# Transfers of the first input pair on two queues, squares of the stream after the last weight cast, and a split power of scales in a one-core decoder trunk

## The chip, the core and the metric

The kernel runs on one core of a Trainium2 chip. The metric is the device time in microseconds (us) of one execution, lower is better; it is given as the median of three runs. The engines are named as in the profile: PE is the matrix engine (TensorE), PEld its weight loads, DVE the VectorE, ACT the ScalarE, POOL the GpSimd engine, and SP the engine that only issues transfers here. Each engine executes its instructions in the order in which they stand in its queue. SP and ACT both issue DMA transfers, each on a queue of its own.

## What is computed

A two-layer decoder trunk on a sequence of 256 positions, width 1024. The first layer (DSA) projects the normalized stream with `w_in`, cuts the result into latents, and lets an indexer pick for each query the top 64 keys; everything that the change touches lies in these lines:

```python
h = rmsnorm(x, g_attn[0])
proj = h @ w_in                       # 1024 x 456
c_q, c_kv, k_idx, w_idx = split(proj, [256, 384, 448])
c_q, c_kv, k_idx = rmsnorm of each
q_idx = einsum(c_q, w_q_idx)
rel = relu(einsum(q_idx, k_idx)); score = einsum(w_idx, rel)   # causal mask
sel = top_k(score, 64)                # then attention over the chosen latents
x = x + attention @ w_o; x = x + sq_relu_mlp(rmsnorm(x), w_up, w_down)
# second layer (NSA), its MLP, final rmsnorm
```

## The kernel before

All 256 positions are held in on-chip memory, transposed (`xT`: 8 row blocks of 128 by 256). The program is one straight line: input projection, indexer, top-k, attention, output projection, MLP, the second layer. The order of the instructions on each engine is set by a scheduler with a cost model of its own; only instructions wrapped in `pin` keep the order in which they are written, and `behind(a, b)` puts `a` after `b`. Tiles come from pools; transfers signal completion on eight counters that are used in turn, so that the ninth transfer waits until the first has landed, and so on.

The **input stage** (L206 to L283) runs over four pairs j of row blocks. For each, SP brings a pair of `xT` (256 KB, written x0 to x3 below) and a pair of weight blocks `win{j}_raw` (456 KB, w0 to w3). SP's queue holds: `vec` (26 KB of gains, L207), then x0, w0, x1, w1, x2, w2, x3, w3 (L252, L254), `cst`, the next weights, `biasT`, and then the output weights `wo_raw`.

- Pair 0 is used in plain fp32: ACT scales x0 by the gain (`xg0`, L258, two instructions), and PE makes four matmuls of 456 columns (two rows each in the trace), called the first projection below.
- Pairs 1 to 3 are split into a high and a low part. ACT makes the high part of the stream pair (`xgh`, L260) and of the two weight blocks (`win`, L266, two instructions); DVE makes the low parts (`xgl` L261, `win` L267). PE makes 12 matmuls of 456 columns for each pair (`mm3`), 36 in all, called the split projection.
- ACT then squares the four stream pairs (`sqs`, L278), two of them ahead of the casts of w3. DVE adds the squares (L280) behind its last low part, POOL makes `Sx`.

At the start PE runs ten matmuls of `ones` by `ones` (`warm_ps`, 20 rows) and one small matmul `ups` for a bias table, which goes by DVE (`usb`), an ACT transfer (`udr`, L231) and an SP transfer (`biasT`, L301) to the attention.

After the projection DVE copies its query part (`zc`, L314), PE transposes it, DVE and ACT form the sums of squares `ss`, and POOL raises six of them per position to the power -0.5 in one instruction (`scs`, L355): columns 0 and 1 for the query and key/value latents, column 2 for the indexer keys. Another power follows (L356). With column 2 DVE scales the keys (`kd`, L362), PE transposes them (`tk`), DVE writes `kiT`, PE makes the indexer products `ix`, and DVE the scores and the top-k.

Of the kernel before, what the change touches and what calls it, by code (L numbers as in the profile page):

```python
# [22 lines left out]
F32 = mybir.dt.float32  # L23
F32R = mybir.dt.float32r
AF = mybir.ActivationFunctionType
OP = mybir.AluOpType
# [4 lines left out]
P, T, D, KT = 128, 256, 1024, 8  # L31
# [19 lines left out]
def trunk(ctx: ExitStack, tc: tile.TileContext, I, out):  # L51
    nc = tc.nc
    const = ctx.enter_context(tc.tile_pool(name="const", bufs=1))
    big = ctx.enter_context(tc.tile_pool(name="big", bufs=10))
    rawp = ctx.enter_context(tc.tile_pool(name="raw", bufs=5))
# [5 lines left out]
    def new_phase(name):  # L61
        nonlocal work
        phase.close()
        work = phase.enter_context(tc.tile_pool(name=name, bufs=2, reuse_waits="tile"))
# [5 lines left out]
    def bank(name, acc=False):  # L70
        if acc:
            return psA.tile([P, 512], F32, tag="acc", name=name)
        return psB.tile([P, 512], F32, tag="ps", name=name)

    def bigt(shape, dt, name):
        return big.tile(shape, dt, tag="big", name=name)

    def wk(tag, bufs, shape, name, dt=F32):
        return work.tile(shape, dt, tag=tag, name=name, bufs=bufs)
# [4 lines left out]
    def k4(shape, name, dt=F32):  # L84
        return rawp.tile(shape, dt, tag="raw", name=name)
# [4 lines left out]
    def f(ap):  # L90
        return ap.bitcast(F32)

    def mm(ps, a, b, start, stop):
        return nc.tensor.matmul(ps, a, b, start=start, stop=stop, skip_group_check=True)  # L94

    def mm3(ps, ah, al, bh, bl, start, stop):
        mm(ps, ah, bh, start, False)
        mm(ps, ah, bl, False, False)
        mm(ps, al, bh, False, stop)

    def behind(ins, prev):

        tc.add_manual_dep(ins.ins, prev.ins.name,
                          mybir.DependencyInfo(mybir.DependencyClass.NoSync, mybir.DependencyReason.DATA),
                          reason="order")
# [46 lines left out]
    def pin(ins):  # L152

        return tc.keep_in_program_order(ins)
# [48 lines left out]


    new_phase("workA")
    vec = const.tile([P, NV], F32, name="vec")  # L206
    nc.sync.dma_start(vec, I["vecs"])  # L207
    mhalf = const.tile([P, 4], F32, name="mhalf")
    nc.gpsimd.memset(mhalf, -0.5)
    ones = const.tile([P, P], F32, name="ones")  # L210
# [3 lines left out]
    wps = bank("warm_ps")  # L214
# [7 lines left out]

    ups = bank("ups")
    mm(ups[:H, :256], relb, oneh, True, True)
    for n in range(2):
        mm(wps[:, :P], ones, ones, True, True)
    usb = wk("pe", 4, [H, 384], "usb")
    nc.gpsimd.memset(usb[:, :P], NEG)
    nc.vector.tensor_copy(usb[:, P - 1:P + 255], ups[:H, :256])
# [9 lines left out]

    xT = bigt([P, KT, T], F32, "xT")
    xgh = bigt([P, KT, T], F32R, "xgh")
    xgl = bigt([P, KT, T], F32R, "xgl")
    proj = [bank(f"proj{i}", acc=True) for i in range(2)]
# [1 line left out]
    sqs = bigt([P, 4, 2, T], F32, "sqs")  # L247
    cst = const.tile([P, NC_], F32, name="cst")
    lo_last = None
    for j in range(4):  # L250
        pair = slice(2 * j, 2 * j + 2)
        nc.sync.dma_start(xT[:, pair], I["xT"][:, pair])  # L252
        raw = rawp.tile([P, 2, 456], F32, tag="raw", name=f"win{j}_raw")
        nc.sync.dma_start(raw.rearrange("p a m -> p (a m)"), I["a_w_in"][j])  # L254
        if j == 0:
            xg0 = k4([P, 2, T], "xg0")
            for k in range(2):
                nc.scalar.activation(xg0[:, k], xT[:, k], AF.Copy, scale=vec[:, V_GA + k:V_GA + k + 1])  # L258
        else:
            xh = nc.scalar.copy(xgh[:, pair], xT[:, pair])  # L260
            nc.vector.tensor_sub(xgl[:, pair], xT[:, pair], f(xgh[:, pair]))  # L261
            w = wp.tile([P, 2, 1024], F32R, tag="w", name=f"win{j}")
            wh, wl = (w[:, s, :912].rearrange("p (a m) -> p a m", a=2) for s in range(2))
            for a in range(2):
                g = vec[:, V_GA + 2 * j + a:V_GA + 2 * j + a + 1]
                hi_last = nc.scalar.activation(wh[:, a], raw[:, a], AF.Copy, scale=g)  # L266
                lo_last = nc.vector.scalar_tensor_tensor(wl[:, a], raw[:, a], g, f(wh[:, a]),  # L267
                                                         op0=OP.mult, op1=OP.subtract)
        for i in range(2):
            for a in range(2):  # L270
                k = 2 * j + a
                if j == 0:
                    mm(proj[i][:, :456], xg0[:, k, i * P:(i + 1) * P], raw[:, a], k == 0, False)
                    continue
                mm3(proj[i][:, :456], xgh[:, k, i * P:(i + 1) * P], xgl[:, k, i * P:(i + 1) * P],
                    wh[:, a], wl[:, a], False, k == KT - 1)
    for j in range(4):
        behind(nc.scalar.activation(sqs[:, j], xT[:, 2 * j:2 * j + 2], AF.Square), hi_last if j > 1 else xh)  # L278
    for j in range(1, 4):
        sq_last = nc.vector.tensor_tensor(sqs[:, 0], sqs[:, 0], sqs[:, j], op=OP.add)  # L280
        behind(sq_last, lo_last)
# [60 lines left out]
    ss = const.tile([P, 2, 4], F32, name="ss")  # L342
# [9 lines left out]
                                               accum_out=ss[:, i, j:j + 1])  # L352
        nc.vector.tensor_scalar(ss[:, i, :3], ss[:, i, :3], epv[:, i:i + 1], None, op0=OP.add)
    scs = const.tile([P, 2, 4], F32, name="scs")
    nc.gpsimd.tensor_tensor(scs[:, :, :3], ss[:, :, :3], mhalf[:, None, :3].to_broadcast([P, 2, 3]), op=OP.pow)  # L355
    pin(nc.gpsimd.tensor_tensor(scs[:, :, 3], msx, mhalf[:, :2], op=OP.pow))  # L356
    sc = [scs[:, i] for i in range(2)]
    indexer_queries(0)
# [513 lines left out]
    for kv in range(2):  # L872
        ps = bank(f"kc{kv}")
        for g in range(G):
# [7 lines left out]
                                      op=OP.mult)  # L882
# [84 lines left out]
    raw = rawp.tile([P, 1024], F32, tag="raw", name="wg_raw")  # L967
# [419 lines left out]
```

## Time and profile before

| | |
|---|---|
| median of three runs | 593.86 us (593.1 to 595.12) |
| profiled execution, device time | 593.29 us |
| its span, first to last instruction | 591.5 us |
| PE busy in the span | 577.2 us (98%) |
| DVE, ACT, POOL busy | 364.2, 320.4, 159.1 us |
| transfers | 103.97 MB, 176 GB/s over the span |

The profile has a page with busy times, 40 slices and the chain of work that ended last; the trace behind it gives every instruction with its start, its duration and what it waited for. Times in it are us from the start of the span. A row of the timeline reads: start, duration, engine, line, operation, out<-in, shape, count, and in brackets how long the engine was idle before and what ended that.

### The profile page before, as it was taken

To read this page: it belongs to the slowest core of one execution; us is meant where nothing else is said; L and a number is where in the kernel's file an instruction comes from. 1 tells how busy PE (TensorE), PEld (TensorE's weight loads), DVE (VectorE), ACT (ScalarE), POOL (GpSimd) and SP (SyncE) were. 2 spreads that over 40 slices of the span, in tenths; PEclk is the share of its full clock that TensorE was granted. 3 is DMA by queue.
4 is the path that set the end of the run, shared out by engine and by line. 5 is a ranking of instruction groups with operands and counts; after the bars stand their busy time and mean duration, and the time that the engine had idled before them with its cause. 6 is when DMAs were issued, how large, how long until landed. Compare 5 with 4: busy or idle time off the path is not lost.

```text
span 591.5 us, 10852 instructions
## 1 busy us (share of the span) xinstructions
PE 577.2 (98%) x4170; PEld 542.9 (92%) x4170; DVE 364.2 (62%) x612; ACT 320.4 (54%) x580; POOL 159.1 (27%) x225
## 2 busy tenths in 40 slices
PE   8899999999999999999999999999999999999995
PEld 6787899999999999999968999999899999999994
DVE  3897399544474444547897877639845444454523
ACT  6656666444444454436866878637544545454423
POOL 0155457010101011015530076808310110011012
PEclk9999999999999999999999999999999999999998
DMA  8911447765546656543499943314866665656201
GB/s 300 345 47 61 149 176 235 249 194 178 179 145 212 181 178 190 180 164 113 160 308 304 327 139 102 97 49 138 287 205 186 181 191 169 180 180 203 77 0 71
DMA packets 30475, 103.97 MB, mean 176 GB/s; under 512 B 3632, under 2 KB 5464, under 8 KB 30296
## 3 DMA queue, kind: packets, MB, share of 16 engines
q1 hardware_dynamic: 30024, 102.45, 53.7%
q10 hardware_dynamic: 400, 0.83, 0.5%
q8 instruction: 32, 0.52, 0.4%
q14 instruction: 19, 0.16, 0.1%
HBM read 102.21 MB, written 1.06 MB: 175 GB/s over the span
## 4 chain that ended last, share of the span: by engine, by line
PE 84%; DVE 9%; issue 2%; DMA 2%; ACT 1%; POOL 1%; SPq 1%; POOLq 0%; ACTq 0%; DVEq 0%
PE y L94 30%; PE u L94 28%; PE nq L94 4%; PE yb L94 3%; PE ya L94 3%; PE kk L94 2%; PE npo L94 2%; PE kc L94 1%; PE nl L94 1%; DVE c L903 1%; DMA win_raw<-in_a_w_in 1%; PE v L94 1%; PE co L94 1%; PE ix L94 1%; DMA wv_raw<-in_kvV 1%
## 5 line engine op out<-in xcount | busy, mean ns | idle before, releaser
L142 DVE TENSOR_TENSOR dn<-dn_raw,dn 128x1024 fp32r<-128x1024 f32 x64 | 80.6, 1260 | 99.2 <-ACT dn L141 99.2
L645 POOL TENSOR_TENSOR us<-ur 128x256 f32<-128x256 f32 x64 | 45.4, 711 | 282.0 <-ACT ur L642 282.0
L142 DVE TENSOR_TENSOR up<-up_raw,up 128x1024 fp32r<-128x1024 f32 x64 | 81.9, 1280 | 44.6 <-ACT up L141 44.6
L141 ACT CAST up<-up_raw 128x1024 fp32r<-128x1024 f32 x64 | 67.0, 1048 | 60.0 <-PE y L94 58.5
L94 PE MATMUL u<-h1h,up 128*128 128x256 f32 x512 | 97.0, 284 | 0.6 <-DVE up L142 0.6
L94 PE MATMUL y<-uu,dn 128*128 128x256 f32 x768 | 97.0, 283 | 0.3 <-DVE uu L647 0.3
L94 PE MATMUL u<-h0h,up 128*128 128x256 f32 x512 | 96.7, 283 | 0.0
L94 PEld LDWEIGHTS y<-uu,dn 128*128 128x128 f32 x768 | 94.2, 192 | 0.5 <-DVE uu L647 0.5
L94 PE MATMUL y<-dn,uu 128*128 128x512 f32 (+1 forms) x396 | 92.5, 384 | 0.0
L94 PEld LDWEIGHTS y<-dn,uu 128*128 128x128 f32 x396 | 71.1, 189 | 13.0
L94 PEld LDWEIGHTS u<-h1h,up 128*128 128x128 f32 x512 | 81.5, 191 | 1.6 <-DVE up L142 0.8
L642 ACT ACTIVATE ur<-u 128x256 f32<-128x256 f32 x64 | 24.6, 384 | 107.2 <-PE u L94 107.2
L94 PEld LDWEIGHTS u<-h0h,up 128*128 128x128 f32 x512 | 81.7, 192 | 0.0
L94 PE MATMUL u<-h1l,up 128*128 128x256 f32 x256 | 72.5, 283 | 0.0
L94 PE MATMUL u<-h0l,up 128*128 128x256 f32 x256 | 72.2, 283 | 0.0
L141 ACT CAST dn<-dn_raw 128x1024 fp32r<-128x1024 f32 x64 | 66.7, 1042 | 7.2 <-PE y L94 3.0
L94 PEld LDWEIGHTS u<-h1l,up 128*128 128x128 f32 x256 | 49.0, 191 | 0.9
L94 PEld LDWEIGHTS u<-h0l,up 128*128 128x128 f32 x256 | 49.1, 192 | 0.0
L647 DVE TENSOR_TENSOR uu<-us,uu 128x256 fp32r<-128x256 f32 x64 | 29.1, 455 | 8.1 <-POOL us L645 8.1
L646 ACT ACTIVATE uu<-ur 128x256 fp32r<-128x256 f32 x64 | 26.7, 417 | 0.1
L94 PE MATMUL ya<-oT,wo 128*128 128x256 f32 x192 | 25.2, 288 | 0.3 <-DVE oT L591 0.3
L94 PE MATMUL nq<-ah,wq 128*128 128x256 f32 x128 | 24.9, 286 | 0.0
(300 smaller groups left out, 966.8 us busy)
## 6 DMA issues: line engine op xcount, KB each, us to landing
up_raw<-in_w_up SPq DMA_DIRECT2D x64, 512.0 KB, 3.7
dn_raw<-in_w_down SPq DMA_DIRECT2D x64, 512.0 KB, 3.7
c1raw<-in_cmp_w SPq DMA_DIRECT2D x16, 512.0 KB, 4.9
wo_raw<-in_a_w_o SPq DMA_DIRECT2D x8, 512.0 KB, 4.1
wq_raw<-in_b_w_q SPq DMA_DIRECT2D x8, 512.0 KB, 5.9
wn_raw<-in_b_w_o SPq DMA_DIRECT2D x8, 512.0 KB, 4.9
wk_raw<-in_kvT SPq DMA_DIRECT2D x4, 512.0 KB, 3.6
wc_raw<-in_kvT SPq DMA_DIRECT2D x4, 512.0 KB, 3.6
```

The lines of the kernel that those rows point to most:

```text
L94: return nc.tensor.matmul(ps, a, b, start=start, stop=stop, skip_group_check=True)
L141: ins = [hi(w[:, 0, :C], raw[:, :C]) if hi else nc.scalar.copy(w[:, 0, :C], raw[:, :C]), (lo or nc.vector).tensor_sub(w[:, 1, :C], raw[:, ...
L142: (lo or nc.vector).tensor_sub(w[:, 1, :C], raw[:, :C], f(w[:, 0, :C]))]
L642: nc.scalar.activation(r, ps[:, :T], AF.Relu)
L645: nc.gpsimd.tensor_tensor(s, r, r, op=OP.mult)
L646: nc.scalar.activation(u[:, 0], r, AF.Square)
L647: nc.vector.tensor_sub(u[:, 1], s, f(u[:, 0]))
L903: lo = nc.vector.tensor_sub(w4[:, :, 1], r4, f(w4[:, :, 0]))
```

## The change

- x0 becomes the first transfer on SP. w0 becomes the first on ACT, and `vec` the second on ACT, behind it. In the order of the changed program SP then holds x1, x2, x3, and behind them w1, w2, w3.
- On PE three `ones` matmuls are pinned behind `ups` (two stood there before).
- All four squares stand behind the last high cast of w3 (`hi_last`).
- POOL's power is split: first the keys' column 2 for both halves (two values per partition), then columns 0 and 1 (four values), then the one of L356 as before.

```diff
+    xT = bigt([P, KT, T], F32, "xT")
+    pin(nc.sync.dma_start(xT[:, 0:2], I["xT"][:, 0:2]))
+    raw0 = rawp.tile([P, 2, 456], F32, tag="raw", name="win0_raw")
+    pin(nc.scalar.dma_start(raw0.rearrange("p a m -> p (a m)"), I["a_w_in"][0]))
     vec = const.tile([P, NV], F32, name="vec")
-    nc.sync.dma_start(vec, I["vecs"])
+    pin(nc.scalar.dma_start(vec, I["vecs"]))
...
-    for n in range(2):
-        mm(wps[:, :P], ones, ones, True, True)
+    for n in range(3):
+        pin(mm(wps[:, :P], ones, ones, True, True))
...
-        nc.sync.dma_start(xT[:, pair], I["xT"][:, pair])
-        raw = rawp.tile([P, 2, 456], F32, tag="raw", name=f"win{j}_raw")
-        nc.sync.dma_start(raw.rearrange("p a m -> p (a m)"), I["a_w_in"][j])
+        raw = rawp.tile([P, 2, 456], F32, tag="raw", name=f"win{j}_raw") if j else raw0
+        if j:
+            nc.sync.dma_start(xT[:, pair], I["xT"][:, pair])
+            nc.sync.dma_start(raw.rearrange("p a m -> p (a m)"), I["a_w_in"][j])
...
-        behind(nc.scalar.activation(sqs[:, j], xT[:, 2 * j:2 * j + 2], AF.Square), hi_last if j > 1 else xh)
+        behind(nc.scalar.activation(sqs[:, j], xT[:, 2 * j:2 * j + 2], AF.Square), hi_last)
...
-    nc.gpsimd.tensor_tensor(scs[:, :, :3], ss[:, :, :3], mhalf[:, None, :3].to_broadcast([P, 2, 3]), op=OP.pow)
+    pin(nc.gpsimd.tensor_tensor(scs[:, :, 2], ss[:, :, 2], mhalf[:, :2], op=OP.pow))
+    pin(nc.gpsimd.tensor_tensor(scs[:, :, :2], ss[:, :, :2], mhalf[:, None, :2].to_broadcast([P, 2, 2]), op=OP.pow))
```

The scheduler orders the changed program anew. The places where its order differs and that matter below are these.

On ACT, in the input stage, before (`xg` is the scaled x0, `xgh` the high part of x1, x2, x3 in turn; `win_134`, `win_156`, `win_178` are the high parts of w1, w2, w3):

```order
L218 DMA relb<-in_rel_bias 32x8
L213 ACTIVATE warm<-ones 128x1
L220 DMA oneh<-in_onehot 32x256
L258 ACTIVATE xg_122<-xT,vec 128x256 x2
L260 CAST xgh<-xT 128x512
L231 DMA udr<-usb 8x383
L266 ACTIVATE win_134<-win_raw,vec 128x456 x2
L266 ACTIVATE win_156<-win_raw,vec 128x456 x2
L278 ACTIVATE sqs<-xT 128x512 x2
L266 ACTIVATE win_178<-win_raw,vec 128x456 x2
```

and after:

```order
L210 DMA win_raw<-in_a_w_in 128x912
L212 DMA vec<-in_vecs 128x52
L265 CAST xgh<-xT 128x512
L263 ACTIVATE xg_123<-xT,vec 128x256 x2
L265 CAST xgh<-xT 128x512 x2
L271 ACTIVATE win_135<-win_raw,vec 128x456 x2
L271 ACTIVATE win_157<-win_raw,vec 128x456 x2
L236 DMA udr<-usb 8x383
L271 ACTIVATE win_179<-win_raw,vec 128x456 x2
L283 ACTIVATE sqs<-xT 128x512 x4
```

The cast of x1 now stands ahead of the scaling of x0; the casts of x2 and x3 stand ahead of all weight casts; `udr` stands two weight pairs later.

On PE, from the start, before (`proj_115` and `proj_116` are the two halves of the positions; the rows with `xg` are the first projection):

```order
L94 MATMUL warm_ps<-ones 128x128 x10
L94 MATMUL ups<-oneh,relb 8x256
L94 MATMUL proj_115<-win_raw,xg_122 128x456 x2
L94 MATMUL proj_116<-win_raw,xg_122 128x456 x2
L94 MATMUL proj_115<-win_134,xgh 128x456
```

and after:

```order
L94 MATMUL warm_ps<-ones 128x128 x8
L94 MATMUL proj_119<-win_raw,xg_123 128x456
L94 MATMUL proj_120<-win_raw,xg_123 128x456
L94 MATMUL ups<-oneh,relb 8x256
L94 MATMUL warm_ps<-ones 128x128 x3
L94 MATMUL proj_119<-win_135,xgh 128x456
```

Eight instead of ten `ones` matmuls lead; `ups` and three more moved between the first projection (its four matmuls alternate between the halves, of which two are shown) and the split projection.

On DVE, between the scaled keys and the first score, before (`wuq` are the low parts of two weights):

```order
L362 TENSOR_SCALAR kd<-proj_116,scs 128x128
L370 TENSOR_SCALAR widx<-proj_115,scs 128x8
L372 TENSOR_SCALAR widx<-widx,scs 128x8
L367 TENSOR_SCALAR kiT<-tk,vec 64x256 x2
L379 TENSOR_TENSOR wuq_285<-wuqr_207,wuq_285 128x1024
L465 SCALAR_TENSOR_TENSOR score_345<-rel_291,widx,cst 128x128
```

and after:

```order
L369 TENSOR_SCALAR kd<-proj_120,scs 128x128
L374 TENSOR_SCALAR kiT<-tk,vec 64x256 x2
L386 TENSOR_TENSOR wuq_287<-wuqr_208,wuq_287 128x1024
L377 TENSOR_SCALAR widx<-proj_119,scs 128x8
L379 TENSOR_SCALAR widx<-widx,scs 128x8 x2
L472 SCALAR_TENSOR_TENSOR score_347<-rel_293,widx,cst 128x128
```

The small `widx` instructions moved from between `kd` and `kiT` to behind the two `wuq` subtractions.

## Rows read from the trace of the kernel before

**Rows 1.** Windows, a long stretch: window, length, busy us of PE, PEld, DVE, ACT, POOL

```profile
60.00:300.00 240.00, 239.74 (x1948) 236.66 (x1947) 144.95 (x170) 124.52 (x190) 58.47 (x73) 1.00 0.58 183
```

**Rows 2.** Chain of waits in order of time, input stage: start, us, what

```profile
4.20 6.37 DMA win_raw<-in_a_w_in
10.59 1.25 ACT win L266 x2
12.35 1.05 ACT sqs L278 x2
15.30 0.61 DVE sqs L280
17.49 0.67 DVE zc L314 x2
```

**Rows 3.** Timeline of PE and PEld, start to the end of the split projection

```profile
1.02 4.14 PE L94 MATMUL warm_ps<-ones 128*128 128x128 f32 x20 [1.02 <-POOL ones L211]
5.09 0.59 PE L94 MATMUL ups<-oneh,relb 32*8 32x256 f32 x2
6.34 3.30 PE L94 MATMUL proj<-win_raw,xg 128*128 128x456 f32 x8 [0.66 <-DMA win_raw<-in_a_w_in]
9.45 1.20 PE L94 MATMUL proj<-win,xgh 128*128 128x456 f32 x3
...
10.18 0.19 PEld L94 LDWEIGHTS proj<-win,xgh 128*128 128x128 f32 x1 [0.43 <-DVE win L267]
...
17.11 0.37 PE L94 MATMUL proj<-win,xgl 128*128 128x456 f32 x1
```

**Rows 4.** Timeline of ACT, input stage

```profile
4.95 0.91 ACT L258 ACTIVATE xg<-xT,vec 128x256 f32<-128x256 f32 x2 [2.27 <-DMA xT<-in_xT]
7.43 0.62 ACT L260 CAST xgh<-xT 128x512 fp32r<-128x512 f32 x1 [1.58 <-DMA xT<-in_xT]
```

**Rows 5.** Timeline of SP, its first two issues

```profile
0.73 0.39 SPq L207 DMA_DIRECT2D vec<-in_vecs  x1
1.18 0.42 SPq L252 DMA_DIRECT2D xT<-in_xT  x1
```

**Rows 6.** Windows, input stage: the last three columns are PE's granted clock, DMA share, GB/s

```profile
2.00:7.43 5.43, 4.77 (x23) 3.73 (x22) 0.57 (x2) 1.57 (x4) 0.00 (x0) 1.00 0.89 266
7.43:12.40 4.97, 4.91 (x19) 3.10 (x18) 3.67 (x6) 4.18 (x8) 0.00 (x0) 1.00 1.04 402
```

**Rows 7.** Timeline from the power on POOL to the first score

```profile
20.22 1.35 POOL L355 TENSOR_TENSOR scs<-ss,mhalf 128x6 f32<-128x6 f32 x1 [1.92 <-DVE ss L353]
21.54 0.70 POOL L356 TENSOR_TENSOR scs<-msx,mhalf 128x2 f32<-128x2 f32 x1
21.61 0.61 DVE L362 TENSOR_SCALAR kd<-proj,scs 128x128 f32<-128x128 f32 x2 [1.54 <-POOL scs L355]
...
22.10 0.50 PE L364 MATMUL tk<-cst,kd 128*128 128x128 f32 x2 [0.71 <-DVE kd L362]
...
22.69 0.99 DVE L367 TENSOR_SCALAR kiT<-tk,vec 64x256 f32<-64x256 f32 x2
...
26.12 0.35 DVE L465 SCALAR_TENSOR_TENSOR score<-rel,widx,cst 128x128 f32<-128x128 f32 x1
```

**Rows 8.** Windows at the program's end, columns as in Rows 1 and 6

```profile
584.00:588.00 4.00, 0.27 (x3) 0.07 (x1) 2.33 (x6) 1.71 (x6) 0.79 (x2) 1.00 0.33 131
588.00:592.00 4.00, 0.00 (x0) 0.00 (x0) 0.00 (x0) 0.00 (x0) 0.00 (x0) 0.52 0.42 137
```

**Rows 9.** Tile views: weight loads of the first `ones` matmuls and of the split projection

```profile
L94 PEld LDWEIGHTS warm_ps<-ones x20: 192/333/338, 1.0 to 4.8; 128*128 128x128 f32 x20
...
L94 PEld LDWEIGHTS proj<-win,xgh x24: 186/187/189, 9.4 to 16.7; 128*128 128x128 f32 x24
```

**Rows 10.** Issue of the bias transfer (us to landing) and its first reader

```profile
biasT<-udr SPq DMA_DIRECT2D x1, 1024.0 KB, 10.1
...
41.54 0.27 DVE L522 CUSTOM_DVE_ANT_0 pe<-lg,biasT 128x128 f32<-128x128 f32 x1
```

More of the change, by code (lines that the diff above doesn't have):

```diff
@@ L238, in bias_keys @@
         return biasT[:, h, :ns][:, ::-1]
-    xT = bigt([P, KT, T], F32, "xT")
     xgh = bigt([P, KT, T], F32R, "xgh")
```

## The prediction

> **What bounds the kernel now.** I read the windows first: between 60 and 300 us PE is busy 239.74 of 240 us [rows 1]. Behind the attention there is no slack that could swallow an early delay or lend an early gain, and the order of the changed program differs from the old one only up to the first scores; so I take it that what the first 26 us gain or lose arrives whole at the end. Next I read the chain of waits through the input stage [rows 2]. It goes from the landing of w2 at 10.57 over ACT's casts, two squares (1.05 us at 12.35) and DVE's additions to the copy `zc` at 17.49. The timeline of PE [rows 3] shows a second chain that ends at the same time: the first projection starts at 6.34 when w0 has landed, the split projection starts at 9.45, and its last row ends at 17.11 + 0.37 = 17.48. Between 6.34 and 17.48 I find one idle time worth naming, 0.43 us before 10.18. So PE and DVE arrive together; taking the squares off DVE's chain alone buys almost nothing, and the stage can only end earlier if the first projection starts earlier. When it starts is the main question.
>
> **Part 1: when the first projection starts.** Before, x0 lands at 4.95, ACT scales it at once, and PE waits for w0 until 6.34 [rows 3, 4]. After, ACT's queue has the cast of x1 ahead of the scaling of x0, so PE waits for x1, for that cast and for half the scaling. x1 landed at 7.43 before [rows 4]. From 2.00 to 7.43 the transfers moved 5.43 x 266 = 1444 KB [rows 6]; what had been issued up to x1 (`vec`, the two bias inputs, x0, w0, x1) is 1052 KB, so x1's last piece came in with 392 KB of later transfers already moved. After the change x0, w0, `vec` and x1 are 1018 KB; if the two queues share the engines and the same 392 KB run ahead, 1410 KB must move, 34 KB or 0.1 us fewer. x0 is issued in the slot of `vec`, at 0.73 instead of 1.18 [rows 5], 0.45 us earlier. So x1 lands near 7.43 - 0.45 - 0.1 = 6.9. `vec` stands behind w0, which is through before x1, and the cast covers it. Then 0.62 for the cast, 0.5 for the first of two scalings (0.91 for both) [rows 4] and about 0.08 of hand-overs: PE starts at 8.1, against 6.34.
>
> **Part 2: PE from there.** The first projection takes 9.45 - 6.34 = 3.11 until the next block can start. `ups` now lies here: 0.59 with its drain, 0.45 until the next instruction. The three `ones` matmuls are six rows; at the start such a row took 4.14 / 20 = 0.21 [rows 3], but with weight loads of 333 ns where the split projection has 187 ns [rows 9], so at full pace I take 0.125 each, 0.75 in all (bounds 0.7 and 1.24). They used to run while PE waited for data; now they lie on the path. The split projection took 17.48 - 9.45 = 8.03; its idle 0.43 closes, since operands are ready early, leaving 7.6. PE ends at 8.1 + 3.11 + 0.45 + 0.75 + 7.6 = 20.0 against 17.48: **2.5 us later**.
>
> What feeds PE must hold. ACT is through with the scaling near 8.5, the casts of x2 and x3 take it to 9.8. w1 is issued only when w0 has landed and comes behind x3: 2.04 MB + 0.39 MB, 1 MB more than at 7.43 before, at 402 GB/s [rows 6] near 9.9 less 0.45, so 9.4. ACT's casts of w1 take 1.25 [rows 2], 9.8 to 11.1; PE wants them at 12.4. w3 follows 0.93 MB or 2.3 us later, 11.8; its casts end near 14 even with the `udr` issue ahead of them, PE wants them at 17.4. ACT, DVE and the queue are covered by over 1 us each. If that cover were gone, each microsecond of lateness would be one on the path.
>
> `udr` is issued about 5 us later, and SP's `biasT` waits for it, with `sel` and the `wo` transfers behind. Issue to landing of `biasT` took 10.1 us, its first reader runs at 41.54 [rows 10]; issued at 17 to 18 rather than 12.45 it lands by 28. I cost this at nothing; the cover is 13 us.
>
> **Part 3: the squares.** DVE's additions follow its last low part, now well before PE ends; the four squares on ACT (0.6 each) are done near 16.5. So `zc` no longer stands behind the additions: its first half can start when the first half of the positions is done, two matmul rows before PE's end. I take 0.25 us earlier relative to PE (0 to 0.4).
>
> **Part 4: the split power.** POOL took 1.35 for six values and 0.70 for two [rows 7]. The keys' two now come first, so `kd` starts 0.65 earlier; PE stood idle 0.71 before `tk`, so `tk` and `kiT` follow it. But DVE went from `kd` to the first score without a pause, 21.61 to 26.12 [rows 7], and the wait for `tk` was filled with `widx` (0.47 between 22.22 and 22.69). `widx` now stands behind `wuq`, and DVE waits instead. Gain 0.65 - 0.47, about 0.15 (0 to 0.6, the upper end if the top-k waits for PE and not for DVE's own work). The other latents' scales come 0.3 us later; their readers stand behind `wuq` or later.
>
> **Sum:** 2.5 - 0.25 - 0.15 = 2.1 us slower. The profiled execution took 593.29 for a span of 591.5, 0.57 below the median of 593.86. I add the difference to the median: 593.86 + 2.1 = 596.0. In general the difference is x1's landing less 4.8.
>
> **Rival: not slower.** The first transfers ran at 266 GB/s, the later ones at 402 [rows 6]. If two queues fill that ramp, 1410 KB at 402 take 3.5 us from 1.55 (2.00 less 0.45): x1 at 5.05, and 594.2. With half of the 392 KB running ahead, x1 is there at 4.6: 593.7. It decides at a landing of 4.8. For: the ramp is slow while one queue leads. Against: in those windows the engines were already 89% occupied [rows 6], which a second issuer does not change.
>
> The Trainium skill's page "DMA: Bandwidth & Descriptors" ("Issuing engines are not separate DMA queues") says of transfers started on several engines that they run on the same 16 DMA engines and that only issue time is saved. By that rule only the 0.45 us of issue remain, which is the 596.0 above. The trace agrees as far as the 89% goes; no run so far has large transfers on both queues.
>
> **Rival: part of it.** x1 between 5.3 and 6.5: 594.4 to 595.6, say 594.9.
>
> **Rival: PE's clock.** Weight loads of the first `ones` matmuls took 333 ns in the median, the last of them 192 [rows 9], though the granted clock reads 1.00 there: PE starts at the lower of its two levels (1.2 GHz) and reaches the higher (2.4 GHz) after some 3.8 us of work. At the end PE stops by 584.3; the granted clock is 1.00 until 588 and 0.52 on average after that [rows 8], so it fell after some 4 us idle. After the change PE has nothing from 1.02 + 16 x 0.21 = 4.4 to 8.1: 3.7 us, at the edge, behind fewer matmuls to raise the clock than before. If it is low, the first projection runs at half pace until the level rises: 3.8 us of half pace cost 1.9, a part of it 1 or so; I take 1.7, 597.7.
>
> The Trainium skill's page "TensorE: Matmul & The Clock Gate" ("HAM oscillation — how this bites in real kernels") says that pauses between bursts of matmuls return the array to half rate. By it this rival would be the forecast; the rows here leave it open.
>
> **How the numbers follow.** Forecast 42% (596.0), clock 33% (597.7), part of it 15% (594.9), not slower 10% (593.7). The range leaves out the last and some of the ends: 594.4 to 598.3, the upper end being the clock rival with x1 at 7.2 and the three matmuls at 1.24. A measurement here can tell about 0.3%, 1.8 us, from no change. Slower than 595.6: the clock rival and two thirds of the forecast's spread, 62%. Faster than 592.1 needs x1 at 3.0, or something not in these rows: 4%. The rest, 34%, is within.
>
> **What would show it.** In the new profile: ACT's first cast of x1 ahead of the scaling, starting near 6.9; the first row of the first projection near 8.1 and its end 3.1 us later (more than 4 us, with weight loads above 300 ns, would be the clock); the split projection without pauses, ending near 20.0; DVE idle about 0.9 before `kd` instead of 1.54; the first score about 1.9 to 2.2 later than 26.12. I am wrong if x1 lands before 5.5, if PE waits again inside the split projection, or if the delay is made up before 60 us.

## The result and the profile after

The changed kernel takes 597.3 us in the median (596.44 to 597.79, 4 runs) against 593.89 us for the kernel before on the same chip (593.1 to 595.12). The ratio is 1.0057, 95% interval 1.0037 to 1.0077: slower by more than the 0.3% that can be told from no change. The profiled execution took 597.07 us for a span of 595.3, 3.78 more than the profiled one of before. One execution of a later kernel, the one with the longer warm-up, took 869.78 us at a mean granted clock of 0.606 and is left out of that kernel's median.

I begin with the timeline of the first 21 us after the change: start, us, engine, line, what, and in brackets the idle time before it with what ended it. Of all engines' rows only those are shown that the reading uses. They answer to [rows 3 to 5].

```profile
0.73 0.42 ACTq L210 DMA_DIRECT2D win_raw<-in_a_w_in  x1
0.73 0.39 SPq L208 DMA_DIRECT2D xT<-in_xT  x1
1.02 3.43 PE L94 MATMUL warm_ps<-ones 128*128 128x128 f32 x16 [1.02 <-POOL ones L216]
1.18 1.36 SPq L258 DMA_DIRECT2D xT<-in_xT  x3
1.18 0.45 ACTq L212 DMA_DIRECT2D vec<-in_vecs  x1
5.76 1.28 SPq L259 DMA_DIRECT2D win_raw<-in_a_w_in  x3
6.58 0.62 ACT L265 CAST xgh<-xT 128x512 fp32r<-128x512 f32 x1 [3.42 <-DMA xT<-in_xT]
6.82 0.15 DVE L430 TENSOR_SCALAR gkvs<-vec 128x1 f32<-128x1 f32 x1 [6.82 <-DMA vec<-in_vecs]
7.10 0.90 ACT L263 ACTIVATE xg<-xT,vec 128x256 f32<-128x256 f32 x2
7.66 4.86 PE L94 MATMUL proj<-win_raw,xg 128*128 128x456 f32 x8 [3.21 <-ACT xg L263]
...
12.44 0.59 PE L94 MATMUL ups<-oneh,relb 32*8 32x256 f32 x2
12.97 0.94 PE L94 MATMUL warm_ps<-ones 128*128 128x128 f32 x6
13.66 0.86 PE L94 MATMUL proj<-win,xgh 128*128 128x456 f32 x3
...
20.99 0.37 PE L94 MATMUL proj<-win,xgl 128*128 128x456 f32 x1
```

ACT waits 3.42 us for x1 and then casts it; only behind that does it scale x0. PE has nothing from the end of the `ones` matmuls (1.02 + 3.43 = 4.45) to 7.66. The first projection starts 7.66 - 6.34 = 1.32 later than before, and then it is slow itself: 7.66 to 12.44 is 4.78 us where it was 6.34 to 9.45, 3.11. That is the second part of the loss, 1.67. `ups` and the three `ones` matmuls lie on the path for 13.66 - 12.44 = 1.22. The split projection has no pause any more: 13.66 to 20.99 + 0.37 = 21.36 is 7.70, 0.33 less than the 8.03 of before. Together 1.32 + 1.67 + 1.22 - 0.33 = 3.88: PE ends at 21.36 instead of 17.48.

Why the first projection is slow is seen in the windows of the same stretch. Columns: window, length, busy us of PE, PEld, DVE, ACT, POOL, then PE's granted clock, DMA share, GB/s.

```profile
5.00:6.00 1.00, 0.00 (x0) 0.00 (x0) 0.00 (x0) 0.00 (x0) 0.00 (x0) 1.00 1.03 349
6.00:7.00 1.00, 0.00 (x0) 0.00 (x0) 0.15 (x1) 0.42 (x1) 0.00 (x0) 1.00 1.02 374
7.00:8.00 1.00, 0.34 (x1) 0.34 (x2) 0.69 (x1) 1.00 (x4) 0.00 (x0) 0.68 0.81 163
8.00:9.00 1.00, 1.00 (x2) 0.49 (x2) 0.46 (x1) 1.00 (x3) 0.00 (x0) 0.50 0.94 306
9.00:10.00 1.00, 1.00 (x2) 0.33 (x1) 0.84 (x2) 0.03 (x1) 0.00 (x0) 0.50 1.00 383
10.00:11.00 1.00, 1.00 (x3) 0.51 (x2) 0.02 (x1) 0.73 (x2) 0.00 (x0) 0.61 0.98 387
11.00:12.00 1.00, 1.00 (x4) 0.39 (x3) 1.00 (x2) 0.81 (x2) 0.00 (x0) 1.00 1.00 378
...
60.00:300.00 240.00, 239.74 (x1961) 237.35 (x1960) 144.87 (x177) 124.31 (x193) 61.12 (x77) 1.00 0.57 180
```

PE's busy time is nothing in two whole windows. Then the granted clock falls: 0.68, 0.50, 0.50, 0.61, which is the lower of its two levels (1.2 GHz) for most of 7 to 11, with 2 matmul rows in a window where there are 4 later. The last row is the long stretch of [rows 1]: 239.74 of 240 us again, so nothing can be made up there.

The chain of waits (start, us, what) says the same in one column. It answers to [rows 2]; `win_raw`, `sqs` and DVE are gone from it.

```profile
1.18 5.38 DMA xT<-in_xT
...
6.58 0.25 ACT xgh L265
...
7.10 0.51 ACT xg L263
...
7.66 4.86 PE proj L94 x8
12.51 0.52 PE ups L94 x2
13.04 0.86 PE warm_ps L94 x6
13.90 7.05 PE proj L94 x34
```

The stretch from the power to the first score, in the order of [rows 7]:

```profile
16.47 2.29 DVE L285 TENSOR_TENSOR sqs<-sqs 128x512 f32<-128x512 f32 x3 [0.30 <-ACT sqs L283]
20.98 0.84 DVE L319 COPY zc<-proj 128x256 f32<-128x256 f32 x2 [2.22 <-PE proj L94]
23.80 0.72 POOL L361 TENSOR_TENSOR scs<-ss,mhalf 128x2 f32<-128x2 f32 x1 [4.22 <-DVE ss L358]
24.50 1.01 POOL L362 TENSOR_TENSOR scs<-ss,mhalf 128x4 f32<-128x4 f32 x1
24.55 0.61 DVE L369 TENSOR_SCALAR kd<-proj,scs 128x128 f32<-128x128 f32 x2 [0.91 <-POOL scs L361]
...
25.59 1.00 DVE L374 TENSOR_SCALAR kiT<-tk,vec 64x256 f32<-64x256 f32 x2 [0.42 <-PE tk L371]
...
29.60 0.35 DVE L472 SCALAR_TENSOR_TENSOR score<-rel,widx,cst 128x128 f32<-128x128 f32 x1
```

DVE's additions are done at 18.76, 2.60 us before PE ends; `zc` waits another 2.22 for PE, and it starts 0.38 before PE's end instead of 0.07. POOL's first power starts 23.80 - 21.36 = 2.44 behind PE's end, before 20.22 - 17.48 = 2.74: 0.30 gained. From that power to the first score it is 5.80, before 5.90: 0.10 gained. So the first score comes 3.88 - 0.30 - 0.10 = 3.48 later, as the rows say (29.60 against 26.12), and the end 3.78 later.

### The profile page after: what moved, and what is told of

The parts are those of the page before. It is cut to its first block, busy times and chain, and to the rows that moved or that the text cites. A ratio compares the mean times of both kernels' runs of the same rounds, so it can differ in the third digit from the quotient of the medians.

```text
span 595.3 us, 10855 instructions
## 1 busy us (share of the span) xinstructions
PE 578.6 (97%) x4172; PEld 543.5 (91%) x4172; DVE 363.6 (61%) x612; ACT 320.1 (54%) x580; POOL 159.6 (27%) x226
## 3 DMA queue, kind: packets, MB, share of 16 engines
q10 hardware_dynamic: 688, 1.33, 0.7%
## 4 chain that ended last, share of the span: by engine, by line
PE 85%; DVE 9%; issue 2%; ACT 2%; POOL 1%; DMA 1%; POOLq 0%; ACTq 0%; SPq 0%; DVEq 0%
PE y L94 30%; PE u L94 28%; PE nq L94 4%; PE yb L94 3%; PE ya L94 3%; PE proj L94 2%; PE kk L94 2%; PE npo L94 2%; PE kc L94 1%; PE nl L94 1%; DVE c L910 1%; PE v L94 1%; PE co L94 1%; DMA xT<-in_xT 1%; DVE h0l L160 1%
## 5 line engine op out<-in xcount | busy, mean ns | idle before, releaser
L94 PE MATMUL nq<-ah,wq 128*128 128x256 f32 x128 | 24.9, 286 | 0.0
```

## The experiments

The theory after this reading was that the loss has three parts, in this order of size: the clock that falls while PE waits for x1; the later start of the first projection; and `ups` with three `ones` matmuls on the path. The rivals were a loss that is the transfers' alone (a longer warm-up would give nothing), and a cost of the squares or of the power. In the table the ratio compares all executions of the two kernels but the one left out above, and is not the quotient of the two medians.

| kernel | median us | before beside it | ratio | 95% interval |
|---|---|---|---|---|
| the changed kernel again | 597.56 | 593.38 | 1.0061 | 1.0041 to 1.0080 |
| + longer warm-up | 595.03 | 593.38 | 1.0023 | 1.0008 to 1.0038 |
| + scaling ahead of the cast | 596.77 | 593.38 | 1.0054 | 1.0035 to 1.0074 |
| - three `ones` matmuls | 596.2 | 593.38 | 1.0040 | 1.0028 to 1.0052 |
| + `vec` first, scaling first, warm-up | 594.39 | 593.35 | 1.0016 | 1.0005 to 1.0028 |
| the same, transfers alternating, no three matmuls | 593.89 | 593.58 | 1.0002 | 0.9991 to 1.0012 |
| before + squares | 593.25 | 593.35 | 0.9993 | 0.9980 to 1.0007 |
| before + power | 592.47 | 593.35 | 0.9986 | 0.9970 to 1.0002 |
| before + both | 593.08 | 593.58 | 0.9990 | 0.9979 to 1.0002 |
| before + both + longer warm-up | 592.7 | 593.58 | 0.9985 | 0.9974 to 0.9996 |
| before + both + `vec` on ACT + warm-up | 592.96 | 593.35 | 0.9992 | 0.9978 to 1.0007 |

**The changed kernel once more**, unaltered.

> The changed kernel once more, unaltered, for a second execution's trace. Theory (late start, low clock in the first projection, small work put on PE's path): 597.3 us; the first projection starts near 7.7 and again takes 4.5 to 6.2 us instead of 3.1, even if the mean granted clock of the run is 0.997 and not 0.994 (then the clock had not risen at all before it). Rival (the low clock was an accident of one execution): the first projection takes 3.1 us and the time is about 595.6 in runs with 0.997.

597.56 us. In its profile x1's cast starts early enough for the first projection to start at 7.24, and still it takes 5.02 us. So the low pace is there in both profiled executions. It comes about a little differently, as PE's weight loads show:

```profile
8.11 0.19 PEld L94 LDWEIGHTS proj<-win_raw,xg 128*128 128x128 f32 x1 [0.19 <-issue]
8.67 0.34 PEld L94 LDWEIGHTS proj<-win_raw,xg 128*128 128x128 f32 x1 [0.37 <-ACT xgh L265]
```

The first rows of the projection run at full pace here, and the clock falls only when PE has been at work again for about 1 us (the window 8 to 9 has a granted clock of 0.65, the next two 0.50), behind an idle time of 2.44.

**A longer warm-up.** Fourteen `ones` matmuls instead of eight at the start, nothing else.

```diff
-    for n in range(8):
+    for n in range(14):
...
```

> The changed kernel with 14 instead of 8 matmuls of ones ahead of the first projection, so that PE idles for 1 to 2 us instead of 3.2; nothing else moves. Theory: the first projection still starts at 7.6 to 7.7 (it waits for data), takes 3.1 to 3.3 us instead of 4.8, and everything behind it is 1.5 to 1.7 us earlier: 595.6 to 595.8 us. Rival (the clock does not hang on PE's idle time here): first projection 4.8 us, 597.3 us.

PE's timeline of this kernel:

```profile
1.02 4.90 PE L94 MATMUL warm_ps<-ones 128*128 128x128 f32 x28 [1.02 <-POOL ones L216]
...
7.25 3.33 PE L94 MATMUL proj<-win_raw,xg 128*128 128x456 f32 x8 [1.33 <-ACT xg L263]
```

And the first projection of the unaltered kernel in the run above:

```profile
7.24 5.02 PE L94 MATMUL proj<-win_raw,xg 128*128 128x456 f32 x8 [2.44 <-ACT xg L263]
```

Both start at 7.24 or 7.25, so the pair shows the clock by itself: 3.33 us against 5.02, a difference of 1.69, and the two profiled executions took 595.03 and 596.77, 1.74 apart. The idle time of PE ahead of it is 1.33 instead of 2.44, behind 28 rows instead of 16. The medians are 2.5 apart, 0.8 more than the pair of traces gives. The rival (transfers alone) falls: not one transfer was changed.

**Scaling ahead of the cast.** ACT scales x0 and only then casts x1.

```diff
-                nc.scalar.activation(xg0[:, k], ...
+                xg_last = nc.scalar.activation(xg0[:, k], ...
...
             xh = nc.scalar.copy(xgh[:, pair], xT[:, pair])
+            behind(xh, xg_last)
```

> The changed kernel with the cast of x1 put behind the scaling of x0 on ACT. Theory: the gains vec, which landed at 6.82 behind w0, are now the last thing waited for; PE starts at 7.35 instead of 7.66, 0.3 us gained, 597.0 us. Rival (the cast ahead of the scaling was the whole delay): the scaling starts at 5 us, PE at 5.8 with w0, 1.9 us gained or more, 595.4 us.

ACT's scaling and the first projection:

```profile
6.50 0.91 ACT L263 ACTIVATE xg<-xT,vec 128x256 f32<-128x256 f32 x2 [3.35 <-DMA vec<-in_vecs]
7.06 5.02 PE L94 MATMUL proj<-win_raw,xg 128*128 128x456 f32 x8 [2.58 <-ACT xg L263]
```

Freed of x1, the scaling waits for `vec`, and it starts at 6.50, 0.60 earlier than in the profile of the changed kernel. The median fell by 0.8, within the spread of the two sets. The 26 KB of gains behind w0 on ACT's queue are the next thing that is late: undoing the order of the cast alone gives back little.

**Without the three `ones` matmuls** between `ups` and the split projection.

```diff
-    for n in range(3):
-        pin(mm(wps[:, :P], ones, ones, True, True))
```

> The changed kernel without the three matmuls of ones between ups and the split projection. Theory: they took 0.86 us on PE's path; the split projection starts 0.7 to 0.9 us earlier, 596.5 us. Rival (the operands of w1 are not ready that early, or the clock falls without them): no gain, 597.3 us.

```profile
7.39 6.07 PE L94 MATMUL proj<-win_raw,xg 128*128 128x456 f32 x8 [2.59 <-ACT xg L261]
13.39 0.59 PE L94 MATMUL ups<-oneh,relb 32*8 32x256 f32 x2
13.92 0.90 PE L94 MATMUL proj<-win,xgh 128*128 128x456 f32 x3
```

From `ups` to the split projection it is now 13.92 - 13.39 = 0.53 where it was 1.22: the three matmuls cost 0.69, as the trace of the changed kernel had them. The median fell by 1.36 against the changed kernel beside it, 0.67 more than that. This trace, whose own execution took 597.28 us, shows a third course of the clock: all eight rows of the first projection are slow, 6.07 us.

```profile
12.12 0.34 PEld L94 LDWEIGHTS proj<-win_raw,xg 128*128 128x128 f32 x1 [0.42 <-issue]
```

Weight loads take 0.33 us in the median of the `ones` rows and still 0.34 in this one, the last of the first projection, and the granted clock reads 1.00 in every window up to 16. So no fall is recorded here: the clock had not risen before the first projection at all, behind 16 `ones` rows. The mean granted clock of an execution points to two kinds, with a fall at the start and without one. Of the changed kernel's six executions beside this one, two at 0.995 took 596.77 and 596.92 and three at 0.997 took 597.64 to 597.85; of the twelve here, nine at 0.994 to 0.996 took 595.28 to 596.34, and the profiled one is at 0.998. Kind against kind the difference is 0.5 to 0.7, about what the trace has, so the 0.67 and the 0.8 of the longer warm-up may be a different mix of the two. That isn't shown: of the kind without a fall only this execution of the new order has a trace, and two more of the twelve, at 0.997, took 594.73 and 596.02.

**The gains first, the scaling first, the longer warm-up.** Of ACT's two first transfers `vec` goes ahead of w0; the two edits above (`behind(xh, xg_last)`, 14 `ones` matmuls) stand too.

```diff
+    vec = const.tile([P, NV], F32, name="vec")
+    pin(nc.scalar.dma_start(vec, I["vecs"]))
     raw0 = rawp.tile([P, 2, 456], F32, tag="raw", name="win0_raw")
     pin(nc.scalar.dma_start(raw0.rearrange("p a m -> p (a m)"), I["a_w_in"][0]))
-    vec = const.tile([P, NV], F32, name="vec")
-    pin(nc.scalar.dma_start(vec, I["vecs"]))
```

> The changed kernel with vec ahead of w0 on ACT, the cast of x1 behind the scaling, and 14 matmuls of ones so that the clock holds. Theory: PE starts with w0 at 6.0 to 6.2 and its first projection takes 3.1; the split projection then waits for w1, whose first cast ended near 10.9 to 11.2 in the changed kernel because x2 and x3 are ahead of it on SP: split projection from 11.0, with waits for low parts, about 1.2 us later in all than the kernel before, 594.6 us. Rival (only the first projection's start counts): split projection from 10.4 without a wait, 594.0 us or less.

```profile
4.40 0.91 ACT L263 ACTIVATE xg<-xT,vec 128x256 f32<-128x256 f32 x2 [1.26 <-DMA vec<-in_vecs]
7.06 3.30 PE L94 MATMUL proj<-win_raw,xg 128*128 128x456 f32 x8 [0.58 <-DMA win_raw<-in_a_w_in]
```

`vec` is there at 4.40 and the scaling with it, but now PE waits for w0, which lands at 7.06, 0.72 later than in the kernel before (6.34, [rows 3]), though it is issued earlier. On SP's queue x0 to x3 are all issued by 2.6, ahead of w1; that w0 shares the engines with them there and didn't before is my reading, and not tested by itself. 594.39 is close to what the sum asked for; the place was another.

**The same with alternating transfers and without the three matmuls.** SP's order is x1, w1, x2, w2, x3, w3 again:

```diff
-            nc.sync.dma_start(xT[:, pair], I["xT"][:, pair])
-            nc.sync.dma_start(raw.rearrange("p a m -> p (a m)"), I["a_w_in"][j])
+            pin(nc.sync.dma_start(xT[:, pair], I["xT"][:, pair]))
+            pin(nc.sync.dma_start(raw.rearrange("p a m -> p (a m)"), I["a_w_in"][j]))
```

> The changed kernel with what cost it time taken out one by one: the gains vec ahead of w0 on ACT's queue, the cast of x1 behind the scaling of x0, SP's later transfers alternating again (x1, w1, x2, w2, x3, w3), the three ones matmuls behind ups gone and six more pairs of ones matmuls at the start. With vec first and the cast behind the scaling the first projection started at 7.06 with a wait for w0; with alternating issues fewer bytes stand ahead of w0's end, so I expect w0 near 6.5, the first projection at 6.5 to 7.0, the split projection 0.55 behind the end of it, its end near 18.0, the second selection mask near 44.7, and 593.2 in all (592.6 to 594.0), as the kernel before. If the rest of the loss is not in the order of the first transfers, it stays near 594.4.

```profile
1.02 6.21 PE L94 MATMUL warm_ps<-ones 128*128 128x128 f32 x28 [1.02 <-POOL ones L216]
...
7.07 3.23 PE L94 MATMUL proj<-win_raw,xg 128*128 128x456 f32 x8
```

593.89 us, no difference from the kernel before that can be told, and at the upper side of what was expected. The first projection starts no earlier, at 7.07, but for another reason: it has no idle time before it. The 28 `ones` rows took 6.21 us in this execution (4.90 with the longer warm-up alone, 5.46 in the run above), so PE was still at them; whether w0 had landed by then can't be seen. With this the loss is accounted for as a whole: transfers alternating and `vec` first, the scaling first, the warm-up and the three matmuls are together worth the 4 us. By itself a price is shown only for the warm-up and for the three matmuls.

**The two small edits on the kernel before.** First the squares:

```diff
-        behind(nc.scalar.activation(sqs[:, j], ...), hi_last if j > 1 else xh)
+        behind(nc.scalar.activation(sqs[:, j], ...), hi_last)
```

> The kernel before with one part of the change: all four squares behind the last cast of w3. Theory (PE and DVE ended the input stage together, so the squares alone buy what PE leaves): the first half of zc starts at 17.1 to 17.2 instead of 17.41, the first score 0.2 to 0.3 earlier than 26.12, 0.2 us gained. Rival (the chain of waits through the squares was the bound): the casts of w3 start 1.05 us earlier and zc with them, 1 us gained.

```profile
17.09 0.85 DVE L314 COPY zc<-proj 128x256 f32<-128x256 f32 x2
...
25.80 0.34 DVE L465 SCALAR_TENSOR_TENSOR score<-rel,widx,cst 128x128 f32<-128x128 f32 x1
```

The copy starts at 17.09 instead of 17.41, the first score comes at 25.80 instead of 26.12: 0.32 earlier in the trace, nothing that the medians can tell (593.25 and 593.35).

Then the power:

```diff
-    nc.gpsimd.tensor_tensor(scs[:, :, :3], ss[:, :, :3], ...)
+    pin(nc.gpsimd.tensor_tensor(scs[:, :, 2], ss[:, :, 2], ...))
+    pin(nc.gpsimd.tensor_tensor(scs[:, :, :2], ss[:, :, :2], ...))
```

> The kernel before with one part of the change: the split power. Theory: kd starts 0.65 us earlier, near 20.95, but DVE then idles 0.4 us before kiT since widx has moved, and the first score starts at 25.9 to 26.1 instead of 26.12: 0.1 us gained. Rival (the keys' scale is on the path with all of its time): first score at 25.5, 0.6 us gained.

```profile
6.53 5.15 PE L94 MATMUL proj<-win_raw,xg 128*128 128x456 f32 x8
...
21.56 0.72 POOL L355 TENSOR_TENSOR scs<-ss,mhalf 128x2 f32<-128x2 f32 x1 [2.59 <-DVE ss L353]
...
27.36 0.35 DVE L466 SCALAR_TENSOR_TENSOR score<-rel,widx,cst 128x128 f32<-128x128 f32 x1
```

From the power to the first score it is 5.80, before 26.12 - 20.22 = 5.90 [rows 7]: 0.1. The first row here is a surprise: in this execution (594.06 us, above its median of 592.47) the first projection of a kernel that has the old order of transfers took 5.15 us instead of 3.30 [rows 3], without any pause of PE ahead of it. So the low pace isn't the changed kernel's alone; it is there in single executions of the old order too.

Both together, with nothing else, and then with four more `ones` matmuls, so that PE works from 1.02 until w0 is there:

> The kernel before with only the squares behind the last weight cast and the power split, no new order of transfers. In the traces the two gained 0.3 and 0.1 us apart; if they add, 593.0 against 593.4 for the kernel before, ratio 0.9993 (within 0.3%: no difference that can be told). The rival, that the squares' earlier end lets the split power's gain of 0.65 through, gives 592.6 or less.

593.08 us against 593.58; in its trace the first score comes at 25.81, 0.31 earlier than before, as much as the squares alone gave. No difference that can be told.

```diff
-    for n in range(8):
+    for n in range(12):
...
```

> The same two edits, with four more pairs of ones matmuls at the start, so that PE works from 1.02 until w0 has landed. If the clock's first rise is what makes single executions of the kernel before differ by 1 to 2 us, the first projection runs at full pace in every one and the median falls to 592.5 with few times above 593.5. If the start of the first projection is only pushed back by the added rows, 593.2 or more.

```profile
1.02 4.88 PE L94 MATMUL warm_ps<-ones 128*128 128x128 f32 x28 [1.02 <-POOL ones L211]
...
6.44 3.30 PE L94 MATMUL proj<-win_raw,xg 128*128 128x456 f32 x8
```

592.7 us, ratio 0.9985, the one interval that ends below 1 (0.9996). PE goes from the `ones` rows over `ups` into the first projection without idle time. Of its 11 times 10 lie at 593.3 or below; of the 12 with both edits alone 7 do, of the 29 of before 7. That fits a clock that rises late in some executions and is made sure by more work; with so few times it isn't shown. The gain, 0.9 us, is under the 0.3% that can be told with confidence.

Last, both edits and 14 matmuls at the start, with `vec` alone moved to ACT's queue, SP's order x0, w0, x1, w1 kept, and `ups`, by the scheduler's order, behind the first projection:

> The kernel before with vec moved from the head of SP's queue to the head of ACT's, SP's order kept (x0, w0, x1, w1, and so on), both the squares and the split power as in the change, 14 matmuls of ones ahead of the first projection and ups behind it. Theory: all transfers are 0.45 us earlier, PE starts at 5.9 instead of 6.34, ups costs 0.45, the squares and the power give 0.3: about 0.4 to 0.8 us faster than the kernel before, 592.8 us. Rival (the start of the stream does not follow SP's issue time): PE starts at 6.3, no gain, 593.4 us.

592.96 us, no difference from before. ACT's scaling starts at 4.45 there, 0.5 earlier than before, but the first projection at 6.24, 0.1 earlier, straight behind the longer `ones` rows, and `ups` (0.52) now lies behind it. Earlier gains brought nothing here; PE was still at the `ones` rows, and the chain of waits goes over w1, which landed at 9.10 (its cast started at 8.72 before). What they bring with fewer `ones` rows isn't tested.

## Why the prediction was right, and where it was not

The forecast was slower, 596.0 in a range to 598.3; the result is 597.3. The sign and the range held for the reason given: PE's first projection starts later since it waits for x1. But of the cases the one that came true is the rival on PE's clock (597.7), to which the prediction gave 33%, and not the likeliest, in which the clock holds (42%). The upper end of the range, from the terms that it names (597.7 + 0.3 + 0.49), would be 598.5 and not 598.3; the result lies within either.

- **x1's landing: 6.9 forecast, 6.56 measured** (cast at 6.58), and the first projection at 7.66 instead of 8.1. The estimate took the same bytes at the old rate less the time of issue. In the stretch from 2.00 to 7.00 the new order moved 303 GB/s where the old moved 256 in the same stretch, 5.00 x 47 = 235 KB more; the earlier issue by 0.45 us explains 0.45 x 303 = 136 KB of it. So x1 came a little earlier than by issue time, 0.35 us, and far less than the 2.1 that the rival "not slower" needed (x1 at 4.8). In three more profiles with this order the cast of x1 starts at 6.16 to 6.31, 0.6 to 0.75 earlier than forecast. In the five profiles of this order the transfers moved 303 to 307 GB/s from 2 to 7 us, in the five with the order of before 253 to 262. That the second queue does it is argued, not tested by itself. The Trainium skill's page "DMA: Bandwidth & Descriptors" ("Issuing engines are not separate DMA queues") says that only issue time is saved; the traces agree in the main and differ by those 0.35 to 0.75 us.
- **`vec` through in time: the cover held, the reason did not.** w0 landed at 5.76, before x1, as the prediction said, but `vec`, 26 KB behind it on the same queue, only at 6.82, after x1. It cost nothing because the cast stood ahead of the scaling anyway; with the cast out of the way it was at once the late one (the experiment with the scaling ahead of the cast).
- **The clock: the step that failed.** The term "3.11 for the first projection" was at full pace. It measured 4.78, 1.67 more; the rival had priced it at 1.7, and the pair of traces with the same start gave 1.69. The rows of the program's end [rows 8], where the clock fell only some 4 us after PE stopped, made me take 3.7 us of idle time for a near miss. Here PE was idle for 3.2 us and the granted clock was at 0.50 in the windows behind it. The Trainium skill's page "TensorE: Matmul & The Clock Gate" ("HAM oscillation — how this bites in real kernels") says that pauses between bursts return the array to half rate; this trace agrees, with those 0.50.
- **How the clock came to be low.** The end of one program was a poor measure: in the changed program PE stops near 588.1, and the granted clock is 0.88 from 588 to 592 and 0.50 after that, which puts its fall some 3 us behind (an estimate from those 0.88). At the start it fell behind idle times of 2.44, 2.58 and 3.21 us, in three profiles, and not behind 1.33. The prediction's other words, "behind fewer matmuls to raise the clock", came true as well: in the run without the three matmuls the same 16 rows left the clock low from the start. So the term failed in two ways, by a fall and by a rise that had not come; which is the more frequent isn't shown.
- **`ups` and the three matmuls: 0.45 + 0.75 forecast, 0.53 + 0.69 measured.** Undoing the three gave 0.69 in the trace. The split projection took 7.70, forecast 7.6: its pause closed as said, and nothing in it waited for data, though ACT's cast of w1 could start only at 10.27 (9.4 forecast).
- **The squares: 0.25 forecast, 0.30 to 0.32 measured**, in the changed kernel and alone. **The power: 0.15 forecast, 0.10 measured** in both; DVE's idle time before `kd` was 0.91 (0.9 forecast), and it waited 0.42 for `tk` instead, as said.
- **`biasT`**: issued at 18.74 (17 to 18 forecast), 6.2 us to landing, so there at 24.9; its first reader runs at 45.03. The cover was 20 us, and it cost nothing.
- **The delay arrives whole**: 3.48 at the first score, 3.78 in the profiled executions, 3.4 in the medians.

With the sum of the prediction at the measured sizes, 1.32 + 1.67 + 1.22 - 0.33 - 0.30 - 0.10 = 3.48. The whole distance to the forecast of 2.1 is the clock (+1.67), against 0.44 for the earlier start, with 0.15 of small terms and rounding.

## What to carry to other kernels

When an edit moves the start of TensorE's first real work, cost the same rows at both levels of the clock and ask what TensorE does until then: here 12 added rows of matmuls on `ones` gave back 2.5 of 4.2 us, more than the order of the cast (0.8) or the three matmuls (1.4) alone. When a small transfer is put behind a large one on the same queue, find the first instruction that reads it: here 26 KB behind 456 KB were there at 6.82, and ahead of them at 4.40. And look for who waits for whom in the order of an engine's queue: a cast that is early in the order and late in its data holds everything that stands behind it.

## What was not expected of the hardware

Small transfers behind w0 on ACT's queue were slow. DMA issues of the changed kernel (KB each, us from issue to landing):

```profile
oneh<-in_onehot ACTq DMA_DIRECT2D x1, 32.0 KB, 5.6
...
relb<-in_rel_bias ACTq DMA_DIRECT2D x1, 1.0 KB, 5.4
```

The 32 KB took 5.6 us to land and the one KB 5.4; in the kernel before, where the one KB was the first on that queue, it took 1.8. `vec` took from its issue at 1.18 to 6.82, 5.6 us, and 2.0 as the first on SP's queue before. As the first on ACT's queue, ahead of w0, it still took 3.7, so the place behind w0 isn't the whole of it.

PE's clock rises at a different time in single executions: the changed kernel's 16 `ones` rows at the start took 3.43 us in one execution and 3.78 in another, 28 rows 4.88 to 6.21 in kernels that begin alike, and eight rows of the first projection 3.30 or 5.15 in the same order of work. In the windows before the first rise the granted clock reads 1.00 in all of them, so there the duration of a row tells the level, not the column. Why the rise comes early or late stays open.

POOL's power took 0.72 us for two values per partition, 1.01 for four and 1.35 for six [rows 7]: each two values more cost some 0.3, so that about 0.4 doesn't grow with the values (an estimate from these three).
